# Sliding-window attention: scaling, bias and row maximum in one VectorE instruction per head, and a later place for the third output weights' casts

## The chip, the cores and the metric

The kernel runs on one core of a Trainium2 chip. A core has five engines with queues of their own: TensorE (PE in the profile, with its weight loads shown as PEld), VectorE (DVE), ScalarE (ACT), GpSimd (POOL) and SyncE (SP), which here issues most of the DMAs. Each engine takes the instructions of its queue in order, and waits for other engines through semaphores. Working memory is SBUF (128 partitions); PE writes its results into PSUM, from where DVE and ACT read them.

The metric is the device time of one execution in microseconds (us). The kernel before was run three times: 2181.92, 2186.65 and 2186.86, so its median is 2186.65. One more execution was taken with the profiler on.

## The reference, cut to what matters

One inference step of a one-layer streaming encoder over 1024 prompt positions and 64 sample positions, in fp32. A combined projection feeds a retention branch A and a sliding-window attention (SWA) branch B; both go through output weights, are gated, added and mixed, and cross-attention and a SwiGLU follow. The change lies in branch B and in the output weights of branch A:

```python
def swa_attend(q, k, v, bias, sinks, valid):
    s = einsum('bnqhgd,bnkhd->bnhgqk', q, k) * (SWA_HD ** -0.5)      # 64 ** -0.5 = 0.125
    s = s + bias
    if valid is not None:
        s = where(valid, s, NEG_INF)
    sink = sinks[:, :, None, None]
    m = maximum(max(s, axis=-1, keepdims=True), sink)
    e = exp(s - m)
    p = e / (sum(e, axis=-1, keepdims=True) + exp(sink - m))
    return einsum('bnhgqk,bnkhd->bnqhgd', p, v)

a = (rms_norm(ret_o).reshape(B, S, -1) * silu(ret_g)) @ w_ret_out    # 1024 x 1024 weights
return (sigmoid(gate_a) * a + sigmoid(gate_b) * b) @ w_mix_out
```

There are 16 query heads, 17 chunks of 64 queries (16 of the prompt, one of the sample), and each chunk sees at most 192 keys: its own chunk and the two before it.

## The kernel before, in words

The stages follow each other: projections with retention, SWA, merging of the branches, cross-attention, feed-forward, final norm. Activations lie transposed (features on partitions, 1088 positions along the free dimension). An fp32 product is made of three PE passes over a high and a low part of each operand (`mm3`, `multiply`): ACT casts the high part (L123) and DVE subtracts it for the low part (L124).

**SWA** (`swa`) works on halves: one chunk and one half of the heads, so that 128 partitions hold two heads of 64 queries each, and the two key-value groups `v` and two head pairs `i` give four units per half, each with up to 192 keys. The first two chunks have fewer keys: 64 in halves 0 and 1, 128 in halves 2 and 3. `scores` of a half makes eight matmuls into `pss` (L972), a PSUM tile with one buffer, and then:

- DVE scales by 0.125 and adds the bias into `t`: one instruction over all four units (768 elements) where there are 192 keys (L982), two where there are fewer (L985);
- DVE takes the maximum over the keys (L987), and of its negative and the negative sink the smaller one, `nm` (L988);
- DVE forms sink minus maximum in `es` (L991), ACT takes four exponentials with `nm` as bias and sums them into `den` (L993), then the exponential of `es` (L995); DVE adds it to `den` and takes the reciprocal (L996, L997); POOL multiplies (L999, L1004).

`turn` transposes the result on PE into `pp`, ACT and DVE copy it out (`pT`), and `weigh` multiplies by the values (L1040) into `osb`. The main loop runs `weigh(i - 1)`, `scores(i + 2)`, `turn(i)` and then some pieces of filler, and `in_order` ties each to the last matmul, so PE's order is written out by hand.

**Filler** (`filler`) is other work for PE between the halves: two products of the memory values, and then `w_ret_out` with the retention result, in pieces of 12 matmuls of 384 or 320 columns (half a product over one block of output rows `m` and one of three column chunks `c`). The first six products are for `m` = 0 and 1 over all three chunks; `m` = 2 follows, and its first piece is handed out at `i` = 9. A product needs its weights as high and low parts (`unit`: a DMA into `raw`, which has two buffers, then two casts on ACT and two subtractions on DVE into `wq`, which has six), its operand columns `rets` (loaded from `d_gate` into a ring of ten buffers, `ld`, cast and subtracted, written by `later_operands`), and its gate `g`, also in that ring. DVE multiplies the product by its gate (L1201), SP stores it.

**Order of the queues.** Apart from what is tied, a planner that simulates the program orders the instructions of each queue; it moves an instruction ahead when it believes that its inputs are there. `issue_after(x)` binds it: what is traced inside the block and runs on the engine of `x` is queued behind `x` (no wait for `x` to finish). Each call of `scores` leaves a pair in `marks`: the DVE instruction that makes `es` and the ACT instruction that takes its exponential.

The lines in `filler` that place the weights of `m` = 2, before:

```python
if m == 2:
    with tc.issue_after(first):
        units[m] = self.unit(io["w_ret_out"][m], KT)
...
ins = nc.vector.tensor_tensor(out=g[:, :n], in0=ps, in1=g[:, :n], op=ALU.mult).ins
if step == 2:
    first = ins
```

`step` counts pieces, so `first` is the gate multiplication of the first product, on DVE.

Of the kernel before, what the change touches and what calls it, by code (L numbers as in the profile page):

```python
# [13 lines left out]
AF = mybir.ActivationFunctionType  # L14
ALU = mybir.AluOpType
AX = mybir.AxisListType
# [20 lines left out]
NKEY = 192  # L37
# [72 lines left out]
class Kernel:  # L110
# [438 lines left out]
    def bias_table(self):  # L549

        nc, io = self.nc, self.io
        t = self.ra.tile([P, BLK + 16], F32, tag="sf", bufs=1, name="table")
        rb = self.ra.tile([P, 2, BLK], F32, tag="o", bufs=1, name="rb")[:16]
        table, onehot = t[:32, BLK:], t[:32, :BLK]
        self.load(table, io["rel_bias"])
        self.load(onehot, io["c_onehot"])
        pb = self.norm_psum("pb")
        nc.tensor.matmul(pb[:16, :256], table, onehot, start=True, stop=True)
        nc.vector.tensor_copy(rb, pb[:16, :256].unsqueeze(1).broadcast_to([16, 2, 256]))
        self.store(self.d_rb.rearrange("h (i c) -> h i c", c=512),  # L560
                   rb.rearrange("p a b -> p (a b)").unsqueeze(1).broadcast_to([16, 32, 512]))
        row = self.np.tile([P, 16], F32, tag="row", bufs=1, name="row")[:1]
        self.load(row, io["sinks"])
        ps = self.norm_psum("ps")
        nc.tensor.matmul(ps[:, :16], self.ones[:1, :], row, start=True, stop=True)
        for e in range(2):
            rows = slice(e * 64, (e + 1) * 64)
            nc.vector.tensor_copy(self.sinks[rows, :], ps[rows, :16].rearrange("p (a b) -> p a b", b=2)[:, :, e])
        self.minus = self.np.tile([P, 16], F32, tag="row", bufs=1, name="minus")[:, :NPAIR]
        nc.vector.tensor_scalar(self.minus, self.sinks, -1.0, None, ALU.mult)  # L570
# [356 lines left out]
    def swa(self, ctx, fill):  # L927
        nc, tc, io = self.nc, self.tc, self.io
        if True:
# [4 lines left out]
            flat, kT, bias, qTs, sinks = self.flat, self.kT, self.bias, self.qTs, self.sinks  # L934
# [20 lines left out]
            units = [(v, i) for v in range(2) for i in range(2)]  # L955
# [8 lines left out]
            def scores(c, hf):  # L964
                ks, j0, nk = keys(c)
                if hf == 0 and c % 4 == 0 and 0 < c < 13:
                    self.load_queries(qTs, c + 4)
                qT = qTs[c // 4 % 2]
                pss = pw.tile([P, 2, 512], F32, tag="s", name="pss")
                for i in range(2):  # L970
                    for v in range(2):
                        self.last_mm = mm(pss[:, v, i * NKEY:i * NKEY + nk], qT[rows[v], 2 * hf + i, c % 4, :],  # L972
                                          kT[rows[v], ks:ks + nk], start=True, stop=True).ins
                quad = lambda x: x.rearrange("p (v h i) -> p v h i", v=2, h=2)[:, :, hf, :]
                snk = quad(sinks)
                t = sw.tile([P, 2, 2, NKEY], F32, tag="t", name="t")
                ps = pss[:, :, :2 * NKEY].rearrange("p v (i n) -> p v i n", n=NKEY)
                bs = bias.rearrange("p (v h i) n -> p v h i n", v=2, h=2)
                nm = sw.tile([P, 2, 2], F32, tag="nm", name="nm")
                if nk == NKEY:  # L980
                    fl = lambda x: x.rearrange("p v i n -> p v (i n)")
                    nc.vector.scalar_tensor_tensor(fl(t), pss[:, :, :2 * NKEY], 0.125, fl(bs[:, :, hf]), ALU.mult, ALU.add)  # L982
                else:
                    for v in range(2):
                        nc.vector.scalar_tensor_tensor(t[:, v, :, :nk], ps[:, v, :, :nk], 0.125, bs[:, v, hf, :, j0:],  # L985
                                                       ALU.mult, ALU.add)
                nc.vector.tensor_reduce(nm, t[:, :, :, :nk], AX.X, ALU.max)  # L987
                nc.vector.scalar_tensor_tensor(nm, nm, -1.0, quad(self.minus), ALU.mult, ALU.min)  # L988
                den = sw.tile([P, 2, 2], F32, tag="den", name="den")
                es = sw.tile([P, 2, 2], F32, tag="es", name="es")  # L990
                ready = nc.vector.tensor_tensor(out=es, in0=snk, in1=nm, op=ALU.add).ins  # L991
                for v, i in units:
                    nc.scalar.activation(t[:, v, i, :nk], t[:, v, i, :nk], AF.Exp, bias=nm[:, v, i:i + 1],  # L993
                                         accum_out=den[:, v, i:i + 1])
                self.marks.append((ready, nc.scalar.activation(es, es, AF.Exp).ins))  # L995
                nc.vector.tensor_tensor(out=den, in0=den, in1=es, op=ALU.add)  # L996
                nc.vector.reciprocal(den, den)  # L997
                p, n, e = t.rearrange("p v i n -> p (v i) n")[:, :, :min(nk, P)], min(nk, P), None
                nc.gpsimd.tensor_tensor(out=p, in0=p, op=ALU.mult,  # L999
                                        in1=den.rearrange("p v i -> p (v i)").unsqueeze(2).broadcast_to([P, 4, n]))  # L1000
                if nk == NKEY:
                    e = sw.tile([P, 2, 2, 64], F32, tag="e", bufs=4, name="e")
                    for v in range(2):
                        nc.gpsimd.tensor_tensor(out=e[:, :, v ^ hf, :], in0=t[:, v, :, P:], op=ALU.mult,  # L1004
                                                in1=den[:, v, :].unsqueeze(2).broadcast_to([P, 2, 64]))
                live[c, hf] = t, e
# [45 lines left out]
            n = len(halves)  # L1052
# [103 lines left out]
    def filler(self):  # L1156

        nc, tc, io = self.nc, self.tc, self.io
        if True:
            ld, rets = self.ld, self.rets  # L1160
            self.first_low()
            us, h = self.first_units, H - 1
            for t in range(2):
                ps = self.dense_psum()
                for k in range(KT):
                    x = self.ms[k][:, :, t * P:(t + 1) * P]
                    self.mm3(ps[:, :256], x[:, 0], x[:, 1], *us[k // 4][k % 4], k == 0, k == KT - 1)
                    if k == 3:
                        yield
                o = ld()[:, :256]  # L1170
                with tc.high_priority():
                    self.values_out = nc.scalar.mul(o, ps[:, :256], self.mtok[:, t:t + 1]).ins
                nc.gpsimd.dma_start(self.d_mv[h, :, t, :], o)
                nc.gpsimd.dma_start(io["o_mv"][t * P:(t + 1) * P, h * 256:(h + 1) * 256], o)
                yield
            self.mem.close()
            self.pw2 = self.mem.enter_context(tc.tile_pool(name="pw2", bufs=2, reuse_waits="tile", side="right"))
            with tc.issue_after(self.values_out):
                units = {0: self.first_out, 1: self.unit(io["w_ret_out"][1], KT)}
            order = [(m, c) for c in range(3) for m in range(2)] + [(m, c) for m in range(2, KT) for c in range(3)]  # L1180
            halves = [range(4), range(4, KT)]
            extra = {2: (1, 0), 3: (1, 1), 5: (2, 0), 7: (2, 1)}
            step = 0
            for m, c in order:
                c0, n = CH[c]
                if m not in units:
                    if m == 2:
                        with tc.issue_after(first):
                            units[m] = self.unit(io["w_ret_out"][m], KT)
                    else:  # L1190
                        units[m] = self.unit(io["w_ret_out"][m], KT)
                u, g = units[m], ld()
                self.load(g[:, :n], self.d_gate[1][m, :, c0:c0 + n])
                for ps in self.pieces(u, rets, c0, n):
                    if step in extra:
                        i, j = extra.pop(step)
                        self.later_operands(*CH[i], halves[j])
                    step += 1
                    if ps is None:
                        yield  # L1200
                ins = nc.vector.tensor_tensor(out=g[:, :n], in0=ps, in1=g[:, :n], op=ALU.mult).ins  # L1201
                if step == 2:
                    first = ins
                self.store(self.d_mix[m, :, c0:c0 + n], g[:, :n])
                yield

# [632 lines left out]
```

## Time and profile before

| what | value |
|---|---|
| median of three runs | 2186.65 us |
| the profiled execution | 2187.39 us |
| its span from first to last instruction | 2185.2 us |
| mean granted PE clock | 0.995 |
| before SWA | 0 to 808 us |
| SWA with its filler | 808 to 988 us |
| of these 180 us, PE busy | 173.24 us |
| DVE, ACT, POOL busy in them | 133.01, 109.59, 64.33 us |
| the rest of the kernel | 988 to 2185.2 us, PE busy 1178.88 |

How to read it. The profile is one execution. A row of a timeline gives the start in us from the span's start, the duration in us, the engine, the line of the kernel, the operation, the tile written and the tiles read, the shapes and how many instructions the row merges; square brackets give the idle time of that engine just before it and what ended it. A row of a group gives line, engine, operation, tiles, shapes and count, then the busy us in total and the mean ns of one, then the idle time in front of them. In the tables of stages, PEclk is the granted clock of PE as a share of full speed, and the last two columns are the mean busy share of the 16 DMA engines and the GB/s that they moved. SPq stands for a DMA issued by SP. The tiles carved out of the ring buffers in SWA (`kT`, `bias`, `qTs`, `ld`) all bear the name `swin`.

### The profile page before, as it was taken

How to read it: one execution, taken by the hardware profiler on the slowest of the kernel's cores; microseconds unless marked ns; L12 is line 12 of the kernel's file. 1: busy time of each engine (PE TensorE's matmuls, PEld its weight loads, DVE VectorE, ACT ScalarE, POOL GpSimd, SP SyncE). 2: the span in 40 equal slices, each digit the busy share in tenths (PEclk: the TensorE clock that was granted, in tenths of full speed). 3: DMA queues.
4: the chain of work that ended last, by engine and by line, in shares of the span. 5: the costliest groups of instructions: out<-in, count | busy, mean ns of one | idle time of the engine just before them, and what ended most of it. 6: DMA issues, size and time to landing. Idle time of an engine off the chain costs nothing.

```text
span 2185.2 us, 41707 instructions
## 1 busy us (share of the span) xinstructions
PE 2144.0 (98%) x16389; PEld 2088.9 (96%) x16389; DVE 1566.2 (72%) x2658; ACT 876.4 (40%) x1898; POOL 651.6 (30%) x498
## 2 busy tenths in 40 slices
PE   8999999999999998999999999999999999999997
PEld 8999999999999997889999999999999999999997
DVE  8996968776677658775455555768777776787588
ACT  7343424344344455653233333333322322344243
POOL 1222333332344213340000000014565555514531
PEclk9999999999999999999999999999999999999998
DMA  6434354445244567326443111422333323294333
GB/s 207 157 128 122 109 148 128 133 121 153 103 160 159 171 206 233 124 80 219 121 154 119 43 49 59 146 87 91 122 126 113 104 99 117 93 331 135 127 110 116
DMA packets 181444, 290.83 MB, mean 133 GB/s; under 512 B 40290, under 2 KB 109314, under 8 KB 181250
## 3 DMA queue, kind: packets, MB, share of 16 engines
q1 hardware_dynamic: 176130, 278.18, 39.7%
q10 hardware_dynamic: 4608, 8.36, 1.0%
q8 instruction: 129, 2.11, 0.4%
q0 software_dynamic: 512, 1.64, 0.2%
q14 instruction: 65, 0.53, 0.1%
HBM read 196.95 MB, written 91.16 MB: 132 GB/s over the span
## 4 chain that ended last, share of the span: by engine, by line
PE 78%; DVE 11%; DMA 5%; issue 2%; ACT 2%; POOL 1%; SPq 0%; POOLq 0%; DVEq 0%; ACTq 0%
PE pq L215 16%; PE pq L212 15%; PE pq L213 15%; PE pd L156 7%; PE pd L158 7%; PE pd L157 7%; DVE wq L124 2%; PE pout L1040 1%; PE pss L972 1%; DMA hl<-d_op 1%; DVE u L259 1%; PE pp L1016 1%; DVE T L124 1%; DVE B L124 1%; DMA raw<-w_k 1%
## 5 line engine op out<-in xcount | busy, mean ns | idle before, releaser
L124 DVE TENSOR_TENSOR wq<-raw,wq 128x512 fp32r<-128x512 f32 (+1 forms) x499 | 443.2, 891 | 145.0 <-ACT wq L123 142.9
L123 ACT CAST wq<-raw 128x512 fp32r<-128x512 f32 (+1 forms) x499 | 302.9, 614 | 588.2 <-PE pq L215 210.4
L212 PE MATMUL pq<-T,wq 128*128 128x272 f32 x1832 | 492.1, 288 | 4.9 <-ACT wq L123 3.2
L213 PE MATMUL pq<-T,wq 128*128 128x272 f32 x1832 | 492.9, 289 | 0.0
L213 PE MATMUL pq<-B,wq 128*128 128x272 f32 x1592 | 427.3, 288 | 3.1 <-DVE B L124 2.9
L212 PE MATMUL pq<-B,wq 128*128 128x272 f32 x1592 | 425.9, 288 | 0.7 <-DVE tok L725 0.4
L190 POOL TENSOR_TENSOR raw<-raw 128x512 f32<-128x512 f32 (+1 forms) x59 | 86.5, 1467 | 1030.5 <-DVE rs_r L301 481.0
L215 PE MATMUL pq<-T,wq 128*128 128x272 f32 x1832 | 382.7, 289 | 1.5 <-DVE wq L124 1.5
L212 PEld LDWEIGHTS pq<-T,wq 128*128 128x128 f32 x1832 | 345.0, 188 | 6.8 <-ACT wq L123 3.3
L213 PEld LDWEIGHTS pq<-T,wq 128*128 128x128 f32 x1832 | 344.6, 188 | 1.2 <-issue 1.1
L215 PE MATMUL pq<-B,wq 128*128 128x272 f32 x1592 | 331.5, 289 | 0.0
L213 PEld LDWEIGHTS pq<-B,wq 128*128 128x128 f32 x1592 | 298.8, 188 | 4.5 <-DVE B L124 4.4
L212 PEld LDWEIGHTS pq<-B,wq 128*128 128x128 f32 x1592 | 298.8, 188 | 1.7 <-issue 0.9
L215 PEld LDWEIGHTS pq<-T,wq 128*128 128x128 f32 x1832 | 290.0, 190 | 2.7 <-DVE wq L124 1.8
L215 PEld LDWEIGHTS pq<-B,wq 128*128 128x128 f32 x1592 | 251.5, 189 | 0.5 <-issue 0.4
L259 DVE TENSOR_TENSOR u<-pq,u 128x544 f32<-128x544 f32 x177 | 127.2, 719 | 92.6 <-PE pq L215 92.5
L193 POOL TENSOR_TENSOR raw<-raw 128x512 f32<-128x512 f32 (+1 forms) x59 | 80.8, 1370 | 93.4 <-DVE wq L124 83.5
L598 DVE TENSOR_TENSOR stage<-pq,u 128x544 f32<-128x544 f32 x112 | 80.3, 717 | 36.7 <-PE pq L215 33.9
L191 POOL TENSOR_TENSOR raw<-raw 128x512 f32<-128x512 f32 (+1 forms) x59 | 89.1, 1510 | 3.6
L196 POOL TENSOR_TENSOR raw<-raw 128x512 f32<-128x512 f32 (+1 forms) x59 | 86.0, 1457 | 4.4
L1488 POOL TENSOR_TENSOR stage<-stage,rstd_f 128x544 f32<-128x544 f32 x40 | 63.9, 1608 | 39.1 <-ACT stage L1487 39.1
L156 PE MATMUL pd<-xc,wq 128*128 128x256 f32 (+1 forms) x256 | 74.5, 291 | 0.0
(385 smaller groups left out, 4555.5 us busy)
## 6 DMA issues: line engine op xcount, KB each, us to landing
hl<-d_op SPq DMA_DIRECT2D x85, 272.0 KB, 5.0
d_qkv<-stage SPq DMA_DIRECT2D x44, 272.0 KB, 2.4
d_op<-stage SPq DMA_DIRECT2D x44, 272.0 KB, 2.1
d_op<-ht SPq DMA_DIRECT2D x44, 272.0 KB, 3.1
raw<-w_gate SPq DMA_DIRECT2D x22, 512.0 KB, 3.5
raw<-w_up SPq DMA_DIRECT2D x22, 512.0 KB, 3.5
raw<-w_down SPq DMA_DIRECT2D x16, 512.0 KB, 5.3
d_gate<-stage ACTq DMA_DIRECT2D x28, 272.0 KB, 3.2
```

What stands on the lines that cost most here:

```text
L123: self.last_cast = self.nc.scalar.copy(hi, src).ins
L124: return self.nc.vector.tensor_tensor(out=lo, in0=src, in1=hi.bitcast(F32), op=ALU.subtract).ins
L156: mm(ps, wh, xh, start=start, stop=False)
L157: mm(ps, wh, xl, start=False, stop=False)
L158: self.last_mm = mm(ps, wl, xh, start=False, stop=stop).ins
L190: tt(out=a11, in0=a11, in1=a21, op=sub)
L191: tt(out=a21, in0=a21, in1=a22, op=add)
L196: tt(out=a12, in0=a12, in1=a11, op=sub)
L212: mm(ps[:, c, :HC], w[:, 0, ks], x[:, 0, cs], start=start, stop=False)
L213: mm(ps[:, c, :HC], w[:, 0, ks], x[:, 1, cs], start=False, stop=False)
L215: self.last_mm = mm(ps[:, c, :HC], w[:, 1, ks], x[:, 0, c * HC:(c + 1) * HC], start=False, stop=stop).ins
L259: add = lambda out, a, b: nc.vector.tensor_tensor(out=out, in0=a, in1=b, op=ALU.add)
```

## The change

In `scores`, the four units of a half each get one DVE instruction `tensor_tensor_reduce`. It reads the unit's scores from `pss` and its bias, adds them, multiplies by -0.125, writes the result to `t`, and writes the minimum of all these values and a starting value, the unit's negative sink, to `nm`. So `t` holds the negative of what it held, `nm` the same as before, and the exponential gets a scale of -1. As the bias is now inside the multiplication, the table in DRAM holds eight times the bias: a multiplication by 8 stands in `bias_table` where a copy stood. The scaling, the maximum and the comparison with the sink (L982 or L985, L987, L988) are gone. The new instruction hands its minimum out through an operand of its own, and takes its starting value from a column of SBUF, one per partition.

In `filler`, `first` is now the pair of marks that stands last when the third product is finished. That is after the main loop's `i` = 3, so the pair is that of half 5. The casts of the weights of `m` = 2 on ACT and their subtractions on DVE are queued behind its two members; before, only the subtractions were bound, to the gate multiplication of the first product.

```diff
-        nc.vector.tensor_copy(rb, pb[:16, :256].unsqueeze(1).broadcast_to([16, 2, 256]))
+        nc.vector.tensor_scalar(rb, pb[:16, :256].unsqueeze(1).broadcast_to([16, 2, 256]), 8.0, None, ALU.mult)
...
-                if nk == NKEY:
-                    fl = lambda x: x.rearrange("p v i n -> p v (i n)")
-                    nc.vector.scalar_tensor_tensor(fl(t), pss[:, :, :2 * NKEY], 0.125, fl(bs[:, :, hf]), ALU.mult, ALU.add)
-                else:
-                    for v in range(2):
-                        nc.vector.scalar_tensor_tensor(t[:, v, :, :nk], ps[:, v, :, :nk], 0.125, bs[:, v, hf, :, j0:],
-                                                       ALU.mult, ALU.add)
-                nc.vector.tensor_reduce(nm, t[:, :, :, :nk], AX.X, ALU.max)
-                nc.vector.scalar_tensor_tensor(nm, nm, -1.0, quad(self.minus), ALU.mult, ALU.min)
+                for v, i in units:
+                    u = quad(self.minus)[:, v, i:i + 1]
+                    nc.vector.tensor_tensor_reduce(t[:, v, i, :nk], ps[:, v, i, :nk], bs[:, v, hf, i, j0:], -0.125, u,
+                                                   ALU.add, ALU.min, nm[:, v, i:i + 1])
...
-                    nc.scalar.activation(t[:, v, i, :nk], t[:, v, i, :nk], AF.Exp, bias=nm[:, v, i:i + 1],
+                    nc.scalar.activation(t[:, v, i, :nk], t[:, v, i, :nk], AF.Exp, bias=nm[:, v, i:i + 1], scale=-1.0,
                                          accum_out=den[:, v, i:i + 1])
...
-                        with tc.issue_after(first):
+                        with tc.issue_after(first[0]), tc.issue_after(first[1]):
                             units[m] = self.unit(io["w_ret_out"][m], KT)
...
-                if step == 2:
-                    first = ins
+                if step == 6:
+                    first = self.marks[-1]
```

## The prediction

> **What bounds the kernel now.** I read the page first, then the table of stages around the sliding-window attention (SWA), then the timelines of PE, ACT, DVE and SP inside the one stage that loses time, then the groups by shape for prices. A "half" is one call of `scores`: one chunk, four of its 16 heads on 128 partitions; there are 34, numbered from 0.
>
> ```profile
> span 2185.2 us, 41707 instructions
> PE 2144.0 (98%) x16389; PEld 2088.9 (96%) x16389; DVE 1566.2 (72%) x2658; ACT 876.4 (40%) x1898; POOL 651.6 (30%) x498
> ```
>
> PE is the bound overall. A change on DVE and ACT can win only where PE waits or runs at a lower clock. The table of stages shows where that is (busy us of each engine, then granted clock, DMA share, GB/s):
>
> ```profile
> core 0: us, PE busy (x) PEld busy (x) DVE busy (x) ACT busy (x) POOL busy (x), PEclk, DMA share, GB/s
> 807.00:820.00 13.00, 11.47 (x82) 10.84 (x80) 7.79 (x21) 12.18 (x36) 4.11 (x8) 0.87 0.52 175
> ...
> 825.90:829.90 4.00, 0.10 (x3) 0.08 (x2) 2.12 (x5) 1.78 (x4) 0.00 (x0) 1.00 0.93 344
> 829.90:834.10 4.20, 4.20 (x22) 4.04 (x23) 3.63 (x12) 3.44 (x14) 0.40 (x1) 0.60 0.98 294
> 834.10:842.00 7.90, 7.90 (x57) 6.42 (x56) 7.87 (x16) 5.03 (x17) 2.01 (x2) 0.99 0.73 233
> 842.00:866.00 24.00, 22.23 (x165) 16.39 (x164) 21.28 (x53) 17.92 (x72) 10.19 (x15) 1.00 0.69 209
> ...
> 880.00:980.00 100.00, 100.00 (x763) 80.47 (x762) 74.74 (x180) 61.37 (x237) 39.14 (x64) 1.00 0.32 99
> ```
>
> From 880 on PE is full and DVE has 25 of 100 us free, so nothing is won there. Before 866 PE loses 1.53 at the start, 3.90 at 826, 0.40 of 4.20 in clock right behind that, and 1.77 in 842 to 866; DVE is full from 834 (7.87 of 7.90). The hole at 826, in the timelines of PE, ACT, DVE and SP and in the chain of waits (last row):
>
> ```profile
> 825.62 0.34 PE L158 MATMUL pd<-ret,wq 128*128 128x384 f32 x1
> 829.85 0.72 PE L972 MATMUL pss<-swin,swin 64*128 64x128 f32 x8 [3.90 <-DVE t L985]
> 831.46 0.52 PE L157 MATMUL pd<-ret,wq 128*128 128x384 f32 x1
> 834.27 0.33 PE L157 MATMUL pd<-ret,wq 128*128 128x384 f32 x1
> ```
> ```profile
> 827.10 1.14 ACT L123 CAST wq<-raw 128x512 fp32r<-128x512 f32 x2 [7.82 <-DMA raw<-w_ret_out]
> ```
> ```profile
> 822.90 0.54 DVE L1201 TENSOR_TENSOR swin<-pd,swin 128x384 f32<-128x384 f32 x1
> 827.75 1.29 DVE L124 TENSOR_TENSOR wq<-raw,wq 128x512 fp32r<-128x512 f32 x2 [4.30 <-ACT wq L123]
> 828.96 0.75 DVE L985 SCALAR_TENSOR_TENSOR t<-pss,swin 128x256 f32<-128x256 f32 x2
> ```
> ```profile
> 829.07 0.33 SPq L117 DMA_DIRECT2D raw<-w_ret_out  x1
> 829.51 0.37 SPq L117 DMA_DIRECT2D swin<-d_gate  x1
> ```
> ```profile
> 819.82 7.20 DMA raw<-w_ret_out
> ```
>
> The third output weights (`w_ret_out[2]`) take 7.20 us to land. Their two casts stand at the head of ACT's queue and wait 7.82; their two low parts stand at the head of DVE's queue and wait 4.30 for the casts; behind those stands the scaling of half 2, whose scores PE had long written. `pss` has one buffer, so PE cannot write half 3: 3.90 us. Then PE's 384-column matmuls take 0.52 instead of 0.33, at a granted clock of 0.60.
>
> **Part 1: the casts of the third weights.** The two casts (ACT, 1.14 us) and two low parts (DVE, 1.29) must now stand behind marks of half 5. In the old timeline that is this row, and this is the first use of the weights by PE:
>
> ```profile
> 845.38 0.19 ACT L995 ACTIVATE es<-es 128x4 f32<-128x4 f32 x1
> ```
> ```profile
> 871.44 0.42 PE L156 MATMUL pd<-ret,wq 128*128 128x384 f32 x1
> ```
>
> There are 26 us between them, and 2.4 us of work: late weights aren't the danger. DVE is free at 823.44 (822.90 + 0.54) and can take half 2 5.5 us sooner than 828.96. PE's hole goes: -3.90. The clock goes with it: 4.20 x 0.40 = -1.7 (0 if PE slows for another hole).
>
> What moves along: the load of the weights itself is not ordered by the edit (they bind ACT and DVE), but its `raw` slot comes free only after the low parts, so the next load into it, today at 829.07, moves past some 15 us of SP's queue. Today SP stands still until 829.07 and `d_gate` at 829.51 stands behind it; that goes. The later weights' next user is far beyond 871.44, so this load is hidden by some 20 us; without that cover it would cost a wait like today's 7.82. POOL's queue holds nothing of these weights. The two low parts now fall into 842 to 866, where DVE is full: +1.29 DVE there, ACT's 1.14 fit (17.92 of 24).
>
> **Part 2: one instruction per head.** Prices from the groups by shape:
>
> ```profile
> L982 DVE SCALAR_TENSOR_TENSOR t<-pss,swin 128x768 f32<-128x768 f32 x30 | 28.6, 952 | 5.1 <-PE pss L972 4.9
> L987 DVE TENSOR_REDUCE nm<-t 128x4 f32<-128x768 f32 x30 | 28.3, 943 | 0.0
> L789 DVE SCALAR_TENSOR_TENSOR sf<-pss,rtok,dm 128x256 f32<-128x256 f32 x16 | 7.6, 477 | 2.4 <-PE pss L158 2.3
> L789 DVE SCALAR_TENSOR_TENSOR sf<-pss,rtok,dm 128x128 f32<-128x128 f32 x16 | 5.4, 339 | 0.0
> L988 DVE SCALAR_TENSOR_TENSOR nm<-nm,minus 128x4 f32<-128x4 f32 x34 | 5.7, 168 | 0.6
> L996 DVE TENSOR_TENSOR den<-den,es 128x4 f32<-128x4 f32 x34 | 5.4, 158 | 14.8 <-ACT es L995 14.7
> L985 DVE SCALAR_TENSOR_TENSOR t<-pss,swin 128x128 f32<-128x128 f32 x4 | 1.0, 286 | 0.0
> ```
> ```profile
> L993 ACT ACTIVATION_READ_ACCUMULATOR t<-t,nm 128x1 f32 x136 | 25.4, 187 | 0.0
> ```
> ```profile
> 837.58 0.95 DVE L982 SCALAR_TENSOR_TENSOR t<-pss,swin 128x768 f32<-128x768 f32 x1
> 838.44 1.49 DVE L124 TENSOR_TENSOR ret<-swin,ret 128x384 fp32r<-128x384 f32 x3
> ```
>
> DVE's queue advances 0.09 sooner than a row ends (0.95 long, next start 0.86 on). Removed per half: 0.86 + 0.86 + 0.08 = 1.80. Added: four passes over 192 elements from PSUM with a scalar per partition. L789 is that but for the minimum: 339 + 64 x (477 - 339)/128 = 408 ns. No row of DVE shows an instruction with a second, reduced output; ACT's exponentials show one, as a read-out row of its own (187). I take a read-out at DVE's price for four elements, 158. So 4 x (0.408 - 0.09 + 0.158 - 0.09) = 1.54: -0.26 per half. Lower bound: no read-out and no price for the scalar, 286 + 64 x (952 - 286)/640 = 353, 4 x 0.26 = 1.05: -0.75. Upper bound: two passes per element, 408 + 192 x 1.08 = 615, and 158 with no overlap, 0.773 each, 3.09: +1.29. I take 1.54, since L789 has the same streams, ports and scalar.
>
> [...] Count alone goes from 3 to 8, at 0.07 each +0.35 per half; here the elements streamed fall from 1,536 to 768, which at 1.04 ns is 0.80, and the rows decide for the gain. By the count alone the sum below would be 8 x 0.61 = 4.9 worse, 2185.7 for 2180.8.
>
> Eight halves (2 to 9) lie before 866: 8 x 0.26 = 2.1 us of DVE, less the 1.29 moved in: 0.8 net. The waits of PE that it can reach:
>
> ```profile
> 845.93 0.66 PE L1016 MATMUL pp<-ident,t 128*128 128x128 f32 x4 [0.84 <-POOL t L999]
> 846.89 0.44 PE L1027 MATMUL pp<-ident,e 128*128 128x128 f32 x2 [0.31 <-POOL e L1004]
> ...
> 863.11 1.25 PE L1040 MATMUL pout<-pT,swin 128*64 128x256 f32 x12 [0.61 <-ACT pT L1020]
> ```
>
> I take -0.8 (bounds -1.8 and +1.3). In the other 24 halves only DVE changes; PE, full there, covers it, and each costs nothing up to DVE's 25 free us in 100. At the start there is a loss:
>
> ```profile
> 809.67 0.55 PE L972 MATMUL pss<-swin,swin 64*128 64x64 f32 x6 [0.68 <-DVE t L985]
> ```
> ```profile
> 809.03 0.49 DVE L985 SCALAR_TENSOR_TENSOR t<-pss,swin 128x128 f32<-128x128 f32 x2
> ```
>
> PE's half 1 waits until DVE has read half 0: 0.49 for two instructions. Four of 64 elements, 339 - 69 = 270 each, with read-outs: 4 x (0.18 + 0.07) + 0.09 = 1.1. So +0.6 (bounds +0.2, +1.3). Later the longer hold of `pss` is covered: half 2 is read from 823.4 to 825.0, before PE wants to write at 825.96; if the cover is gone, each half costs what is over.
>
> The exponentials change a constant scale, and can start after the first head instead of after all four; ACT's order stays. The bias table's copy becomes one multiplication of the same shape in the projection stage, one instruction for one. Both 0.
>
> Sum: -3.9 - 1.7 - 0.8 + 0.6 = -5.8. The profiled execution took 2187.39 (span 2185.2 and 2.2 around it), 0.74 above the median of 2186.65: 2181.6 there, 2180.8 as median, -0.27%.
>
> **The rivals.** A: all of PE's loss before 866 goes, since exponentials start a microsecond sooner in each half: 1.53 + 0.13 x 13 = 3.2 at the start (half of it at most, as the start is also bound by the stage before), 3.9, 1.7, 1.8: -9.0, 2177.7; all of it, -10.6, 2176.1. For it: the waits at 845.93 and 846.89 hang on this chain. Against: DVE stays full.
>
> B: DMA takes the hole's place. Its share is 0.93 to 0.98 from 825.9 to 834.1. The last operand of the next product is loaded at 829.51; with 7.20 it lands at 836.7, and PE will want it about 834.9 (5.6 sooner than now):
>
> ```profile
> 840.52 0.42 PE L156 MATMUL pd<-ret,wq 128*128 128x384 f32 x1
> ```
>
> With a microsecond for its cast, 2.8 of wait: -3.0, 2183.6. If PE's clock falls behind such a hole, as the 0.87 of 807 to 820 behind shorter holes suggests, 1.7 more, 2185.3. [...] Against B: the load in front in SP goes away, and this one can be issued sooner.
>
> C: the hole only moves: DVE's low parts meet a wait at their new place of the size of today's 4.30. 5.8 - 4.3 = 1.5 is left: 2185.2. Against: the data have long landed.
>
> D, slower: the per-head instruction is at its upper bound and DVE becomes the bound. Up to 866: 8 x 1.29 = 10.3, plus 1.29 moved in, less 2.7 free (24 - 21.28), is 8.9 lost against 5.6 won, and +1.3 at the start: +4.6. From 880 on the room per half is (100 - 74.74)/21:
>
> ```profile
> 880.00:980.00 100.00, 20.01 (x21) 1.00 0.32 99
> ```
>
> That is 1.20 (L982 alone in that stretch, 21 halves), less than 1.29; 0.09 x 24 is +2.2, in all +6.8: 2193.5. It decides from 0.75 us per head, (1.80 + 1.20)/4.
>
> **How the numbers follow.** Forecast 0.42, A 0.23, B 0.11, C 0.05, D and whatever else overfills DVE 0.19. 0.3% is 6.6 us, about what a measurement of this kernel can tell from no change: its line is 2180.1, inside the forecast's own range of 2178.5 to 2183.0, which splits 0.20 to 0.22. Faster by over 0.3%: 0.20 + 0.23 = 0.43; within: 0.22 + 0.11 + 0.05 = 0.38; slower: 0.19. The range runs from A with all of it and a microsecond for the spread of runs, 2175, to just short of D, 2193.
>
> **What will show it.** Right: no wait of PE for `t` near 826, clock 1.0 from 820 to 842, casts of the third weights near 840 to 850 with no DMA ahead of them, per-head rows of about 0.41 with read-outs, DVE in 880 to 980 near 70. Wrong: per-head rows over 0.6; PE waiting for `ret` or `swin` at 830 to 840; SP standing still before a `raw` load.

## The result, and the profile after

The changed kernel takes 2181.99 us (median of 20 runs, 2178.17 to 2184.89), the kernel before, measured beside it, 2184.97 (20 runs, 2181.21 to 2191.88). The ratio is 0.9985 with a 95% interval of 0.9978 to 0.9991: 3.0 us less, about half of the 5.8 that the prediction's sum gave. The profiled execution took 2183.19, its span is 2181.1. The page's first lines:

```profile
span 2181.1 us, 41848 instructions
PE 2142.3 (98%) x16389; PEld 2089.0 (96%) x16389; DVE 1553.4 (71%) x2824; ACT 876.4 (40%) x1898; POOL 651.7 (30%) x498
```

DVE does 12.8 us less work in 166 more instructions. The table of stages, with the columns of the one before:

```profile
core 0: us, PE busy (x) PEld busy (x) DVE busy (x) ACT busy (x) POOL busy (x), PEclk, DMA share, GB/s
807.00:820.00 13.00, 11.17 (x75) 10.70 (x74) 4.59 (x24) 10.97 (x33) 2.23 (x4) 0.74 0.59 193
...
825.90:829.90 4.00, 3.65 (x27) 3.05 (x25) 2.62 (x14) 2.98 (x13) 0.00 (x0) 1.00 1.06 378
829.90:834.10 4.20, 4.20 (x32) 3.38 (x32) 4.04 (x16) 4.20 (x16) 1.34 (x1) 1.00 1.03 388
834.10:842.00 7.90, 6.50 (x46) 5.59 (x42) 6.49 (x26) 5.32 (x20) 2.96 (x4) 1.00 0.60 198
842.00:866.00 24.00, 23.33 (x180) 18.42 (x179) 21.27 (x78) 17.97 (x66) 10.97 (x15) 1.00 0.79 247
...
880.00:980.00 100.00, 100.00 (x764) 80.52 (x763) 63.18 (x275) 58.35 (x227) 41.20 (x63) 1.00 0.33 102
```

The hole is gone: PE has 3.65 of 4.00 us in the stretch where it had 0.10. From 842 to 866 it loses 0.67 instead of 1.77. But there is a new loss of 1.40 between 834 and 842, where nothing was lost before, and the clock of the start is 0.74 instead of 0.87. The PE waits, from the timeline of PE:

```profile
810.99 1.12 PE L972 MATMUL pss<-swin,swin 64*128 64x64 f32 x8 [1.01 <-DVE nm L982]
827.03 0.41 PE L156 MATMUL pd<-ret,wq 128*128 128x384 f32 x1 [0.35 <-DVE swin L1196]
838.59 0.92 PE L972 MATMUL pss<-swin,swin 64*128 64x192 f32 x8 [1.40 <-DVE nm L982]
845.25 0.44 PE L156 MATMUL pd<-ret,wq 128*128 128x384 f32 x1 [0.18 <-ACT swin L951]
```

The 1.01 was 0.68. The 0.35 and the 1.40 are new, and the 1.40 is a wait for the scores' only PSUM buffer, `pss`: it is given back when the last of the four per-head instructions has read it. What stood ahead of that, in DVE's timeline:

```profile
834.40 2.31 DVE L124 TENSOR_TENSOR ret<-swin,ret 128x384 fp32r<-128x384 f32 x3
836.63 0.41 DVE L982 CUSTOM_DVE_ANT_0 t<-pss,swin,minus 128x192 f32<-128x192 f32 x1
...
837.31 0.55 DVE L124 TENSOR_TENSOR ret<-swin,ret 128x384 fp32r<-128x384 f32 x1
837.78 0.41 DVE L982 CUSTOM_DVE_ANT_0 t<-pss,swin,minus 128x192 f32<-128x192 f32 x1
838.12 0.08 DVE L982 DVE_READ_ACCUMULATOR2_ANT nm<- 128x1 f32 x1
838.12 0.41 DVE L982 CUSTOM_DVE_ANT_0 t<-pss,swin,minus 128x192 f32<-128x192 f32 x1
```

Three low parts of operands, then two heads, a fourth low part, then the other two heads: a half read in four pieces lets other work in between, and PE waits for the last. PE stood ready from 837.18. An estimate from these rows shares the 1.40 out: one instruction of 0.95 from 836.63 on would have left a wait of some 0.46, as DVE came late behind the three low parts; four heads in a row end 0.48 later, and the low part between them adds 0.47. The casts of the third weights now stand at 843.90 and 847.19 (ACT, then DVE), with no transfer ahead of them. The groups by shape, which give the price of the new instruction:

```profile
L982 DVE CUSTOM_DVE_ANT_0 t<-pss,swin,minus 128x192 f32<-128x192 f32 x120 | 42.9, 413 | 6.4 <-PE pss L972 5.1 <-POOL e L999 0.7
L982 DVE DVE_READ_ACCUMULATOR2_ANT nm<- 128x1 f32 x136 | 11.2, 82 | 0.0
```

413 ns was forecast as 408. The read-out was forecast as 158 and is 82, and it costs some 0.02 at most between two heads: in the timeline one head starts 0.34 after the other (837.78, 838.12), where 0.41 less the 0.09 by which the rows of before overlap is 0.32, and the read-out starts with the next head. Four heads are 4 x 0.34 = 1.36 us instead of the 1.80 removed: -0.44 per half, where -0.26 was taken. What counts for the buffer is the end of the last row: 3 x 0.34 + 0.41 = 1.43 us from the start of the first, where the one instruction before took 0.95.

### The profile page after: what moved, and what is told of

It is laid out like the page before. It is cut to its first block, busy times and chain, and to the rows that moved or that the text cites. A ratio compares the mean times of both kernels' runs of the same rounds, so it can differ in the third digit from the quotient of the medians.

```text
span 2181.1 us, 41848 instructions
## 1 busy us (share of the span) xinstructions
PE 2142.3 (98%) x16389; PEld 2089.0 (96%) x16389; DVE 1553.4 (71%) x2824; ACT 876.4 (40%) x1898; POOL 651.7 (30%) x498
## 3 DMA queue, kind: packets, MB, share of 16 engines
q0 software_dynamic: 512, 1.64, 0.2%
```

## The account of the stage

To tell waits from clock, the sliding-window stage of each profiled execution is counted from its first score matmul: over the next 75 us, PE's idle time, and what its busy time loses to the granted clock (busy time multiplied by one less the clock, in steps of 1 us). The stage's length runs to the end of the last `pout`. "Casts alone" and the others are the experiments below. The kernel before was profiled once, so its row is that of one execution.

| kernel | stage, us | PE idle | lost to clock |
|---|---|---|---|
| before | 179.67 | 6.45 | 3.41 |
| changed | 176.01 | 3.57 | 3.20 |
| changed, second profile | 174.09 | 3.42 | 1.71 |
| casts alone | 179.93 | 7.31 | 3.40 |
| casts alone, second profile | 176.18 | 5.36 | 1.71 |
| casts alone, two pieces later | 179.37 | 5.96 | 4.69 |
| heads alone | 175.65 | 5.28 | 1.64 |
| heads alone, second profile | 176.23 | 5.11 | 1.70 |
| first four halves in three steps | 173.38 | 2.92 | 1.64 |
| the same, second profile | 173.25 | 4.08 | 0.00 |
| the same, casts two pieces later | 174.17 | 5.18 | 0.00 |
| per-head work twice, buffer not held | 176.96 | 4.64 | 3.33 |

Less both losses, these stages are 168.7 to 169.8 us long (before: 179.67 - 6.45 - 3.41 = 169.8; changed: 169.2): the change moves losses and hardly the work. The stages before and behind it, which no kernel here changes apart from one instruction of the bias table, scatter from execution to execution by some 5 and 4 us: the first score matmul comes at 804.6 to 809.3, and from the last `pout` to the end it takes 1195.0 to 1199.1. That is why the time of a kernel needs many runs here. In the account most waits repeat to 0.2 us between two profiles of one kernel; those that don't change its idle time by 0.2 to 2.0 us, and the clock's loss does not repeat.

## Experiments

Each ratio is to runs of the kernel before on the same chip at the same time. The four kernels that were measured at two times came out 1.4 to 3.8 us better, against before, at the second, and for three of them the two intervals hardly overlap or do not; so kernels are compared closely only where they were measured together. Together were: casts alone, heads alone, three steps and the load with the buffer held; then the changed kernel, three steps, the load without hold and the split buffer; then casts alone and the two with later casts. Heads alone stood by itself the second time.

### The casts' move alone

```diff
--- before
+++ casts alone
-                        with tc.issue_after(first):
+                        with tc.issue_after(first[0]), tc.issue_after(first[1]):
...
-                if step == 2:
-                    first = ins
+                if step == 6:
+                    first = self.marks[-1]
```

> The kernel before with the casts' move alone; scaling, bias and maximum stay three VectorE steps. Theory (the prediction's sum): the hole of 3.90 us and the slow clock behind it, 1.7, go; the two low parts of 1.29 come into a stretch where VectorE is full and are not paid for by faster heads. So -5.6 + 1.3 = -4.3 against before, 2180.7, no PE wait near 826, and the start of the stage as before (a wait of 0.68, granted clock 0.87 in 807 to 820). Rival 1, the heads give back at the start what the casts' move wins: this kernel is faster than the changed one by the start's loss, about 2 us: 2180 or below. Rival 2, the hole only moves: a new wait of 3 to 4 us stands behind the low parts at their new place, and the time is 2184 to 2185.

Measured: 2186.05 (before 2184.84), ratio 1.0001 (0.9993 to 1.0010). The hole at 826 is gone, and others have come. From the chief waits of PE in the stage:

```profile
PE pd L156 <- ACT swin L951: 2.1, 1, 2.1
PE pd L156 <- ACT swin L1172: 2.1, 1, 2.1
PE pp L1016 <- POOL t L999: 1.2, 1, 1.2
```

> The kernel before with the casts' move alone, once more. Theory: the hole of 3.90 at 826 only moves: the casts (1.14 on ACT) now stand in ACT's queue between the casts for the operands (1.52) and the copies of the turned values (L951), and PE waits for those copies, 2.1 us, with a wait of 1.2 for the scaled exponentials before it; both again, and the time is that of before within 2 us. Rival: that wait was a chance of one execution, and without it the time is 3 to 4 us below before.

Measured the second time: 2183.53 (before 2185.57), ratio 0.9989 (0.9981 to 0.9998). The waits for L951 and for POOL are there again. In the timelines of ACT and of PE:

```profile
837.18 1.52 ACT L123 CAST ret<-swin 128x320 fp32r<-128x320 f32 x4
838.61 1.13 ACT L123 CAST wq<-raw 128x512 fp32r<-128x512 f32 x2
839.65 0.41 ACT L951 COPY swin<-pd 128x128 f32<-128x128 f32 x2
```
```profile
839.95 0.44 PE L156 MATMUL pd<-ret,wq 128*128 128x384 f32 x1 [2.13 <-ACT swin L951]
```

The two casts stand right ahead of the copies that free the dense products' PSUM buffer, behind four casts of operands, and PE waits 2.13 for the copies. Most of what the prediction gave to this edit is not there: -1.1 us as a mean of both ratios (1.0001 and 0.9989, at 2185), against the -4.3 expected, which lies outside both intervals. The wait for L1172 (ACT's scaling of the values at the start) came once only, 2.12 until 817.90, and the slow clock of that execution stands behind it; the second had its slow clock (0.50, from 808.1 to 811.5) in front of this place, and PE has no wait for L1172 there.

### The heads alone

```diff
--- changed
+++ heads alone
-                        with tc.issue_after(first[0]), tc.issue_after(first[1]):
+                        with tc.issue_after(first):
...
-                if step == 6:
-                    first = self.marks[-1]
+                if step == 2:
+                    first = ins
```

> The changed kernel with the casts of the third weights back at their old place; the per-head instructions stay. Theory (the prediction's sum): the hole stays at about 3.9, a little longer as four per-head instructions read half 2 in 1.1 us where two took 0.5 (+0.6); the start costs +0.6; the freed 8 x 0.44 us of VectorE before 866 take at most the 1.8 of waits there. In all -0.6 with bounds -1.8 and +1.3: 2184.4 (2183.2 to 2186.3). Rival 1, the start's loss is larger since PE's clock stays slow for longer behind it: +2, 2187. Rival 2, the per-head instruction takes the hole away by itself: -4, 2181.

> The per-head instructions alone, the third weights' casts at their old place, once more. Theory (the waits of PE repeat, the slow clock does not): 1.01 at the start, 2.20 at the old hole and 1.32 for the scores' buffer again, each within 0.2, in all 4.9 for that buffer; that is 1.2 us less than the waits of the kernel before, and the time lies 0 to 2 us below it, where the first run gave +0.4. Rival: the hole depends on when the weights land and is back at 3 to 4 us; the time is that of before or above.

Measured: 2185.30 (before 2184.84), ratio 1.0002 (0.9992 to 1.0011), and the second time 2182.18 (before 2185.32), 0.9985 (0.9977 to 0.9994); a mean of -1.4 us. The hole, in PE's timelines of the first and of the second:

```profile
829.23 0.72 PE L972 MATMUL pss<-swin,swin 64*128 64x128 f32 x8 [2.20 <-DVE nm L982]
```
```profile
827.78 0.72 PE L972 MATMUL pss<-swin,swin 64*128 64x128 f32 x8 [2.33 <-DVE nm L982]
837.40 0.92 PE L972 MATMUL pss<-swin,swin 64*128 64x192 f32 x8 [0.16 <-DVE nm L982]
```

The hole stays, smaller than 3.90 and not larger by 0.6 as expected. ACT's casts of the weights start 17.15 and 17.34 us after the first score matmul, 18.77 in the kernel before, so the weights landed sooner; why is open. The waits behind 842 are nearly gone (PE busy 23.59 of 24.00 in 842 to 866, both times): that gain is the heads' alone. Whether it comes from the 0.44 us that VectorE saves per half or from exponentials that start after the first head, no run separates. The wait for the scores' buffer at 837 to 839, 1.32 in the first, is 0.16 in the second, so this one does not repeat: the waits for that buffer are 3.9 us in the second where 4.9 was expected, and the time, 3.1 below before, went past the 0 to 2.

By the times alone it can't be told that both edits together bring more than their sum (-1.1 and -1.4 against -3.3 and -3.7, all from the ratios, whose intervals are each 3 to 4 us wide). The waits say so: against the 6.45 of before, the casts alone have 7.31 and 5.36, the heads alone 5.28 and 5.11, both together 3.57 and 3.42.

### The changed kernel again

> The changed kernel once more, beside the others of this call, for a second profile of the same instructions. Theory A: the waits of PE repeat within 0.2 us (1.01 at the start, 0.35, 1.40, 0.18, 0.49 behind it), and the slow clock does not: in the traces so far it is lost in pieces of 1.6 to 1.7 us (half clock for 3.3 us), one or two or none behind the same holes at the start. Rival: the two pieces of slow clock at the start of the changed kernel belong to its wait of 1.01, and are there again, 3.2 us. Time 2182 as before, within 1.5.

Measured: 2181.45 (before 2185.87), ratio 0.9983 (0.9975 to 0.9992). The chief waits of PE in this second profile are those of the first to 0.1 us:

```profile
PE pss L972 <- DVE nm L982: 2.9, 3, 1.4
PE pss L972 <- DVE stage L598: 0.8, 1, 0.8
PE pd L156 <- DVE swin L1196: 0.3, 1, 0.3
PE pd L156 <- ACT swin L951: 0.2, 1, 0.2
```

The clock is not. From 807 to 820 it is 0.74 in the table above and 0.87 here; with the first four halves in three steps it is 0.87 and 1.00 in two executions. The losses in the account are 1.64 to 1.71, about twice that, or none, and once nearly three times that (4.69): pieces of 3.3 to 3.4 us, twice the loss, as the granted clock in them is 0.50 in every profile that has one. In the 75 us of every profile here a slow stretch (one piece, or two in a row, as from 810.7 to 817.5 in the changed kernel's first) begins within a wait of PE or at most 1.5 us behind one, and the same hole has one or none: 2.33 of heads alone has one behind it (0.50 from 828.7), 2.20 in the first execution of the same kernel has none (1.00). Theory A holds.

### The first four halves in three steps

```diff
--- changed
+++ three steps
+                if nk == NKEY:
                     for v, i in units:
...
+                else:
+                    for v in range(2):
+                        nc.vector.tensor_tensor(out=t[:, v, :, :nk], in0=ps[:, v, :, :nk], in1=bs[:, v, hf, :, j0:], op=ALU.add)
+                    nc.vector.tensor_reduce(nm, t[:, :, :, :nk], AX.X, ALU.max)
+                    nc.vector.scalar_tensor_tensor(nm, nm, -0.125, quad(self.minus), ALU.mult, ALU.min)
...
-                    ... bias=nm[:, v, i:i + 1], scale=-1.0,
+                    ... bias=nm[:, v, i:i + 1], scale=-1.0 if nk == NKEY else 0.125,
```

> The changed kernel, but the first four halves (64 and 128 keys) scale, add and reduce in three steps as before; the 30 halves of 192 keys keep the per-head instruction. Theory: what the changed kernel gives back at the start (a wait of 1.01 for 0.68, half 1 scored behind the division of half 0, PE's clock slow until 817.3 instead of 813.6) is owed to the four per-head instructions of 64 keys, and returns: about -2 against the changed kernel, 2180; the wait is 0.68 again and half 1 is scored before 811.5. Rival: the start is set by when the stage before it ends and when its operands land, and the 1.01 is a chance of that execution: within 0.5 us of the changed kernel, with the slow clock as long as there.

> The kernel with the first four halves in three steps and the others per head, once more beside the changed kernel, since its first twelve times were spread from 2180 to 2189. Theory: its stage loses some 0.6 us less in PE waits than the changed kernel (2.9 against 3.6), so the time is 0 to 2 us below the changed kernel. Rival: the start's form does not matter, and it equals the changed kernel within 0.5 us.

Measured: 2183.01 (before 2184.84), ratio 0.9996 (0.9985 to 1.0007); and, measured with the changed kernel, 2180.27 (before 2185.87), 0.9975 (0.9966 to 0.9983), where that has 0.9983 (0.9975 to 0.9992). The start's wait is 0.68 again and half 1's scores are read from 810.52, as expected; but of the 2 us that this was to bring, 1.2 show, inside both intervals. What happens instead, in the second execution of this kernel:

```profile
815.99 0.44 PE L156 MATMUL pd<-ret,wq 128*128 128x384 f32 x1 [0.79 <-ACT swin L1173]
834.20 0.65 PE L1017 MATMUL pp<-ident,t 128*128 128x128 f32 x4 [1.35 <-POOL t L1000]
840.77 0.45 PE L156 MATMUL pd<-ret,wq 128*128 128x384 f32 x1 [0.94 <-ACT swin L951]
```

At full clock (1.00 from 807 to 820) PE reaches the first product of `w_ret_out` early and waits there 0.79 for ACT. What ACT has ahead of L1173 is read from the first execution: casts of 0.51 and 0.60, a table load of 1.28 at 811.80, and eight exponentials of 0.33 to 0.35 from 813.09 on, with L1173 at 815.96. So what the start gains in clock or in its first wait can be given back in part at this one: in this execution ACT sets when these products begin (8.7 us after the first score matmul; in the changed kernel's first execution, behind its slow clock, 11.0 without a wait).

### Each per-head instruction twice, with and without holding the buffer

Both kernels add four more of these VectorE instructions to each half from half 10 on, behind 866. The first repeats each one on the same scores, so that they are read eight times before the buffer is given back; the second gives four that read the bias table in SBUF, and their results are not used.

```diff
--- changed
+++ twice
                     u = quad(self.minus)[:, v, i:i + 1]
+                    for again in range(2 if c >= 5 else 1):
                         nc.vector.tensor_tensor_reduce(...)
```

> The changed kernel with every per-head instruction given twice from half 10 on, that is behind 866 us: 4 x 0.34 = 1.36 us more of VectorE per half. Theory (the prediction: what VectorE does in these halves is covered by PE as long as it has room): room per half is (100 - 63.18)/21 = 1.75 us, more than 1.36; VectorE goes from 63 to about 92 of 100 us in 880 to 980 and the time stays within 1 us of the changed kernel, 2181 to 2183. Rival, a queue that is 92% full delays the next steps well before it is full: PE waits for t, pT or the dense products, and at 0.3 us per half for 24 halves the time is +7, 2189.

```diff
--- changed
+++ twice, not held
+                if c >= 5:
...
+                    with tc.issue_after(ready):
+                        for v, i in units:
+                            nc.vector.tensor_tensor_reduce(junk, bs[:, v, hf, i, :], bs[:, v, hf, i, :], -0.125,
+                                                           quad(self.minus)[:, v, i:i + 1], ALU.add, ALU.min, low[:, v, i:i + 1])
```

> As the run with every per-head instruction given twice from half 10 on (+18 us), with the same 4 x 0.34 us of VectorE per half, but the second four read the bias table in SBUF instead of the scores in PSUM, stand behind the sum of sinks and maxima, and nothing waits for them; the scores' only buffer is given back as early as in the changed kernel. Theory: what cost 18 us is how long the scores' buffer is held, 2.7 us instead of 1.4 per half, not VectorE's load; so this one is within 3 us of the changed kernel, 2181 to 2185, with VectorE as busy as there (85 to 92 of 100 us in 880 to 980). Rival: VectorE's queue is the bound at that load whatever it reads: 2195 to 2203.

Measured: 2200.67 (before 2184.84), ratio 1.0069 (1.0056 to 1.0083), with the buffer held; 2182.83 (before 2185.87), 0.9988 (0.9979 to 0.9997), without. The stretch from 880 to 980, first held, then not held, and the only waits of PE from 866 to 980 in the first (the second has none):

```profile
880.00:980.00 100.00, 88.56 (x656) 70.96 (x654) 85.44 (x398) 58.10 (x203) 32.60 (x56) 0.98 0.28 87
```
```profile
880.00:980.00 100.00, 100.00 (x758) 81.69 (x757) 88.96 (x433) 57.88 (x223) 37.83 (x63) 1.00 0.33 102
```
```profile
PE pss L972 <- DVE nm L983: 11.7, 11, 2.3
```

This is the clearest reading of the study. DVE is busier in the second (88.96) than in the first (85.44), and PE loses nothing in it, and 11.4 us in the first. What costs is not DVE's load but how long a half's reading holds the scores' buffer: 8 x 0.34 = 2.7 us instead of 1.36. In the first the exponentials start later as well, but PE waits for nothing that hangs on them there, only for the buffer. My expectation of the first (within 1 us) was wrong, and so was its rival's reason, the full queue.

### The scores in two PSUM tiles

```diff
--- changed
+++ split
-                pss = pw.tile([P, 2, 512], F32, tag="s", name="pss")
-                for i in range(2):
-                    for v in range(2):
+                pss = [pw.tile([P, 512], F32, tag=f"s{v}", name="pss") for v in range(2)]
+                for v in range(2):
+                    for i in range(2):
...
```

> The changed kernel with the scores in two PSUM tiles of one bank each instead of one of two banks, so that PE can write the first two heads of the next half when VectorE has read two of four. Theory: the waits of PE for the scores' buffer (1.01 at the start, 1.40 at 838.6 in the changed kernel) come from the longer hold by four instructions; each loses 0.4 to 0.7, in all -1 us, 2181. Rival: the waits are for VectorE's place in its queue (subtractions for the operands stand ahead of the heads), the split is worth under 0.3 us, and writing the four heads in another order costs PE as much as it wins.

Measured: 2184.04 (before 2185.87), ratio 0.9993 (0.9982 to 1.0004), 2.6 above the changed kernel measured with it, where 1 us less was expected; the two intervals overlap, so that it is slower is not shown. Both waits shrink, 1.01 to 0.58 and 1.40 to 0.25, in PE's timeline:

```profile
805.79 1.07 PE L972 MATMUL pss<-swin,swin 64*128 64x64 f32 x8 [0.58 <-DVE nm L981]
829.58 0.91 PE L972 MATMUL pss<-swin,swin 64*128 64x192 f32 x4 [0.25 <-DVE nm L981]
```

The first falls by 0.43, two heads of 64 keys at 0.21: that one is the hold. The second falls by more than two heads (0.68), and not for want of low parts in between. The rows of DVE, and the one of PE where it begins this half's scores:

```profile
827.16 0.40 DVE L981 CUSTOM_DVE_ANT_0 t<-pss,swin,minus 128x192 f32<-128x192 f32 x1
...
827.83 1.01 DVE L124 TENSOR_TENSOR ret<-swin,ret 128x384 fp32r<-128x384 f32 x2
828.77 0.41 DVE L981 CUSTOM_DVE_ANT_0 t<-pss,swin,minus 128x192 f32<-128x192 f32 x1
```
```profile
828.41 0.92 PE L972 MATMUL pss<-swin,swin 64*128 64x192 f32 x4
```

Two low parts stand between the heads here, one in the changed kernel; but DVE begins the half 1.25 us before PE wants to write (827.16, 828.41), there only 0.55 (836.63, 837.18). So DVE's place in the queue has moved too, and how much of the 1.15 is the split is not shown.

The gain is lost again in this profile, which is that of the fastest of the twelve runs (2178.90): the score matmuls of 192 keys take 29.4 us of PE instead of 27.6 in their new order, and `pout` waits for ACT four times, 2.1 in all. Counted as in the account, the stage is 176.6 us, with 4.1 of waits to its end and no slow clock: 172.5 without losses, some 3 us more than the others. From the groups of the split kernel and then of the changed one, and the chief waits of the split one:

```profile
L972 PE MATMUL pss<-swin,swin 64*128 64x192 f32 x240 | 29.4, 349 | 0.3 <-DVE nm L981 0.2
```
```profile
L972 PE MATMUL pss<-swin,swin 64*128 64x192 f32 x240 | 27.6, 349 | 1.9 <-DVE nm L982 1.9
```
```profile
PE pout L1034 <- ACT pT L1014: 2.1, 4, 1.1
PE pd L156 <- ACT swin L951: 1.1, 1, 1.1
```

### The casts two pieces later

In both, `step == 6` becomes `step == 8`: once on casts alone, once on three steps.

> As the casts' move alone, but two pieces later: the casts of the third weights stand behind the marks taken at step 8 instead of 6, so that the copies of the turned values go first in ACT's queue. Theory: the wait of 2.1 for the copies (L951) goes or falls below 1.0, and with it a piece of slow clock where one stood behind it: 1 to 3 us below the casts' move at step 6. Rival: ACT is late there for the exponentials of the half itself, not for the casts; the wait stays within 0.3 us of 2.1.

> The kernel with the first four halves in three steps and the others per head, with the casts of the third weights at step 8 instead of 6. Theory: its wait for the copies of the turned values (0.22 and 0.94 in its two profiles) goes; 0 to 1 us below that kernel, 2179.5 to 2180.5, and below both the kernel before and the changed one. Rival: the casts, later by a piece, meet the next such copy or the exponentials there; no gain, 2181 to 2183.

Measured: casts alone at step 8 2184.08 (before 2185.57), ratio 0.9997 (0.9988 to 1.0006), where step 6, measured with it, has 0.9989; three steps with step 8 2181.36 (before 2185.57), 0.9980 (0.9969 to 0.9991). The chief waits of casts alone at step 8:

```profile
PE pp L1016 <- POOL t L999: 3.7, 2, 2.5
PE pd L156 <- ACT swin L951: 1.1, 1, 1.1
```

The wait for L951 falls from 2.1 to 1.1, which fits the two casts (1.14); the rest is ACT's other work. But a wait of 2.5 for POOL's scaled exponentials has come behind it. With casts alone at step 6 POOL waits for DVE's reciprocal in front of them (4.65 until 835.97, 0.64 until 842.88); that it does so here, and that the later low parts are what delays DVE, is the author's estimate and not shown. In the other kernel the wait for L951 goes, and waits for the scores' buffer come (2.1 in two). Step 8 is no better than step 6, where 1 to 3 us less and 0 to 1 less were expected.

No version here beats the changed kernel beyond the intervals; three steps for the first four halves, at 0.9975 beside 0.9983, is the best candidate, and undecided.

## Why the prediction was right or wrong

The time (2181.99 for 2180.8) and the side are right, within 0.3% and inside the range. The sum, -5.8, is not: it is -3.0 and -4.4 at two times. That the time came within 1.2 us is in part luck: the forecast started from a median of three runs, 2186.65, that lay 1.7 above the 2184.97 of twenty, and this covered 1.7 of the 2.8 by which the sum was too large. Nor are 6.6 us the least that can be told from no change, as the prediction took it: twenty runs of each kernel showed 3.0, with an interval of 2.0 to 4.8. By the terms of the sum:

- **The hole, -3.9.** As a wait it went, as predicted, and the 1.14 and 1.29 of casts were hidden at their new place but for 0.18. But it isn't worth 3.9 by itself: with the three old steps the casts' move brings 1.1 and not 4.3, since ACT's casts then hold back the copies at L951 (2.13, of which 1.0 goes where the casts stand later) and POOL's work comes late (1.2). The step that failed in general is "ACT's 1.14 fit (17.92 of 24)": the share of busy time said that there was room, the queue had a copy right behind that PE needed. In the changed kernel the wait is only 0.18 there. Rival C, that the hole moves, is what happens in part without the faster heads, though by ACT's queue and not by the low parts that C named.
- **The clock, -1.7.** The slow stretch behind the hole is gone, but the clock's loss in the stage is 3.20 and 1.71 against 3.41. The mean granted clock of all runs gives a better size: 0.99584 over 31 runs of the changed kernel, 0.99539 over 108 of the one before, so 0.00045 x 2185 = 1.0 us (0.2 to 1.8 by the scatter of these runs). The term was taken from one execution, in which a piece fell on that hole. A piece is 3.3 to 3.4 us at a granted clock of 0.50, 1.64 to 1.71 lost, and which waits have one behind them differs by run: the 3.90 of before had one, and so had 2.33 in one execution of heads alone, while 2.20 in the other had none.
- **The waits of 842 to 866, -0.8.** 1.77 became 0.67: -1.1, inside the bounds. The relief behind it was mis-sized, -0.44 per half for -0.26: the read-out was priced at 158 ns, and its 82 lie inside the next head. So DVE has 63.18 of 100 us in 880 to 980, not near 70. By the prediction's estimate from the count of instructions alone, +0.35 per half, it would have been a loss; 8 instructions for 3 are cheaper here by 0.44 us.
- **The start, +0.6.** The wait went from 0.68 to 1.01, +0.33, inside the bounds. Four heads of 64 keys take less than priced (0.21 apart for 0.25). Half 1's reading now stands behind the sum of half 0's denominators (L991), which waits 6.79 for ACT, from 811 to 818; the prediction left that out, and PE did not need the buffer before 825.
- **The step that failed: "Later the longer hold of `pss` is covered".** I checked it for half 2 and let it stand for all. At half 4, the first of 192 keys, PE waits 1.40 for the buffer, and 0.35 for a product's gate before it: +1.75, not in the sum. PE needs the buffer, not DVE's time: before, a half gave it back after one instruction of 0.95; now after four, 1.43 when nothing comes between them. By the estimate above, this longer hold is some 0.5 of the 1.40, the low part that came in between another 0.5, and DVE's late start behind three low parts the rest; none of the three was in the sum.

Idle time by these terms: -3.90 - 1.10 + 0.33 + 1.75 = -2.9, and the account has 3.57 - 6.45 = -2.9. With the clock's 1.0 that is -3.9, between the two measured differences.

Of the rivals, A needed all waits to go, and B's wait for a late operand is not there, though the DMA share in 825.9 to 834.1 rose to 1.06 and 1.03. D, slower, had the wrong condition: "it decides from 0.75 us per head" came from DVE's room, 1.20 per half. At 2 x 0.34 = 0.68 per head the kernel is already 15.8 us slower than before, by the buffer; and 1.36 more per half that hold nothing cost nothing beyond the intervals (0.9988 beside 0.9983). D lay nearer than its price said, and it would have come from PE's wait, not from DVE being full.

## What to carry to other kernels

When one long instruction that reads PSUM becomes several, look at two sums: the engine's time, and the time until the last read gives the buffer back. With one buffer, the second is on PE's path even where the engine has time free, 14.6 of 100 us in the run with each instruction twice. And a stall taken away is worth what the next one in line leaves of it: read from each queue which instruction stands directly behind the moved work, not the share of time that is free there.

## What was not expected of the hardware

In the changed kernel's profile the VectorE instruction with a reduced output (L982) takes 413 ns for 192 elements with one source in PSUM, mean of 120, and its read-out of 82 ns, mean of 136, starts with the next head, 0.34 us after its own start (837.78, 838.12). And the same kernel with the same waits lost 3.20 and 1.71 us to the clock in two executions, three steps 1.64 and 0.00: in this stage, a difference of 1.7 us between two profiles says nothing about the kernels.
